# All small parts of the split weights made on VectorE: a one-core layer of attention, RWKV-7 and mixture of experts

## The chip, the cores and the metric

The kernel runs on one core of a Trainium2 chip. TensorE (PE) multiplies, VectorE (DVE), ScalarE (ACT) and GpSimd (POOL) work elementwise, and SyncE (SP) issues most of the transfers from HBM. The metric is the device time of one launch in microseconds (us), lower is better.

## The reference

One layer on 256 tokens of width 1024, in float32:

```python
proj = x @ w_in                                   # 1024 x 5408
y_rwkv = rwkv7_time_mix(token_shift(proj[:, :1824], mu), ...)   # 8 heads of 64, scan over 256 tokens
y_attn = moba_attention(q, k, v)                  # 8 heads of 64, one causal block of 256
mixed = sigmoid(gate_a) * (y_attn @ w_attn_br) + sigmoid(gate_r) * (y_rwkv @ w_rwkv_br)
h = layer_norm(ALPHA * x + mixed @ w_out)
out = layer_norm(ALPHA * h + moe_ffn(h))          # 32 experts, 4 a token, 1024 -> 2048 -> 1024
```

## The kernel before

The kernel has two parts. The **front** (the first 300 us) does everything up to the router. The input projection is cut into twenty chunks of 256 columns, n = 1 to 20 (k, r, v, q and k of the attention, its v, and the two gates), the branch weights into four more, n = 21 to 24. Then the **experts** follow: 32 experts, whose 403 MB of weights are streamed from HBM once, in pieces of 1 MB.

A product of the front is made from three: a weight is split into a large part `hi` (rounded to the type fp32r, line 131, on ScalarE) and a small part `lo`, the rest (line 132, a subtraction of 128x1024). `split(n)` does this in two halves, q = 0 and 1, into one of two pairs of slots in turn, so that chunk n waits until chunk n-2 is multiplied out. `mm3` (lines 140 to 142) multiplies hi by hi, hi by lo and lo by hi: 48 matmuls a chunk. Chunks write two PSUM banks in turn (`b_120` in the rows below is the bank that chunk 8 writes, `b_124` chunk 9, `b_128` chunk 10, `b_132` chunk 11, `b_136` chunk 12, `b_155` chunk 13, `b_159` chunk 14, `b_163` chunk 15, `b_167` chunk 16, `b_188` and `b_192` chunks 19 and 20), and a bank is written again only when its result has been read out: for q and k by lines 562 to 567 on VectorE, for the gates by line 589 on ScalarE. `s_45`, `s_49`, `s_53`, `s_122` and `s_157` are the small parts of chunks 4, 5, 6, 10 and 15; `s_121` and `s_156` are the large parts of chunks 10 and 15.

Beside the chunks run: the inverse of 64 triangular blocks (lines 417 and 419, section `inv`, 31 steps on VectorE, each waiting for the last), its way through HBM and back (lines 423 to 432) to the small products of lines 442 and 449; the recurrence over four pieces of 64 tokens (lines 478 to 508); and the softmax in two halves (lines 600 to 627, the exponentials on line 615).

Which engine makes a small part is read from a table: entry n lists the halves that GpSimd makes, and a chunk without entry has its second half there.

```python
ON_POOL = {6: (0,), 4: (0, 1), 2: (), 21: (0, 1), 14: (0, 1), 8: (0,), 15: (), 1: ()}
```

The order of instructions on each engine is made by a scheduler when the kernel is built, from its own estimate of durations and from the offsets in `PRIORITY`, so that another engine for one instruction changes the order of its neighbours too. On the chip each engine takes its instructions in that order and waits at the first that isn't ready. From the first expert on, TensorE's order is that of the code. `mfill` and `mload` (line 671) ask for expert weights whenever a slot of SBUF is free: the slots of the front become free one after the other, as its last chunks are done, and later each expert's when it has been multiplied.

Of the kernel before, what the change touches and what calls it, by code (L numbers as in the profile page):

```python
# [10 lines left out]
FT = mybir.dt.float32  # L11
# [3 lines left out]
OP = mybir.AluOpType  # L15
# [19 lines left out]

ON_POOL = {6: (0,), 4: (0, 1), 2: (), 21: (0, 1), 14: (0, 1), 8: (0,), 15: (), 1: ()}

# [35 lines left out]
def hybrid_kernel(ctx, tc, xt_d, x_d, win_d, w0_d, ups_d, up2_d, par_d, cA_d, cB_d, wbr_d, wout_d,  # L73
# [7 lines left out]
    V, A, PE, G = nc.vector, nc.scalar, nc.tensor, nc.gpsimd  # L81
    cnt = [0]

    def slot(i, shape, dt=FT):
        cnt[0] += 1
        return slots.tile([128] + shape, dt, name=f"s{i}_{cnt[0]}", tag=f"s{i}")
# [11 lines left out]
    def sec(name):  # L98
        old = cur[0]
        if cur[1] is not None:  # L100
            cur[1].__exit__(None, None, None)
        off = PRIORITY.get(name, 0)
        cur[:] = name, tc.high_priority(offset=off) if off else None
        if off:
            cur[1].__enter__()
        return old
# [5 lines left out]
    RAW, HL = {}, {}  # L112

    def load(n):
        if n >= len(chunks):
            return
        kind, i = chunks[n]
        RAW[n] = slot(raw_of.get(n, raws[n % 2]), [2048])
        src = (win_d if kind == "in" else wbr_d)[i]
        for c in (slice(0, 1024), slice(1024, 2048)) if n == 1 else (slice(0, 2048),):  # L120
            nc.sync.dma_start(RAW[n][:, c], src.rearrange("p a b -> p (a b)")[:, c])

    def split(n):

        if n >= len(chunks):
            return
        hi, lo = slot(hls[2 * n % 4], [2048], FR), slot(hls[2 * n % 4 + 1], [2048], FR)
        old = sec("s%d" % n)
        for q in range(2):
            c = slice(1024 * q, 1024 * q + 1024)  # L130
            A.copy(hi[:, c], RAW[n][:, c])  # L131
            (G if q in ON_POOL.get(n, (1,)) else V).tensor_tensor(lo[:, c], RAW[n][:, c], hi[:, c].bitcast(FT), op=OP.subtract)  # L132
        sec(old)
        a = 8 if chunks[n][0] == "in" else 4
        HL[n] = [t.rearrange("p (a b) -> p a b", a=a) for t in (hi, lo)]
        load(n + 2)
# [50 lines left out]
    for q in range(2):  # L187
        c = slice(4 * q, 4 * q + 4)
# [23 lines left out]


    split(1)
    sec("low")
    pl = [bank(i) for i in range(5)]
# [33 lines left out]
    def proj_chunk(n, b, dst, f0, mc):  # L250
        split(n + 1)
        ps = bank(b, (2, T))
        for h in range(2):
            proj_fm(ps[:, h], n, 128 * h)
            shift(dst[:, f0 + h], ps[:, h], mc + h)
# [4 lines left out]
    for f2 in range(2):  # L260
        pw, pa = bank(2 + 2 * f2, (2, T)), bank(3 + 2 * f2, (2, T))
        for ff in range(2):
            f = 2 * f2 + ff
            c = slice(128 * f, 128 * f + 128)
# [10 lines left out]
    for f in range(4):  # L275
        c = slice(128 * f, 128 * f + 128)
# [161 lines left out]
    for pr in range(2):  # L438
        lo, hi = slice(64 - 64 * pr, 96 - 64 * pr), slice(96 - 64 * pr, 128 - 64 * pr)
# [5 lines left out]
    for pr in range(2):  # L445
        lo, hi = slice(64 - 64 * pr, 96 - 64 * pr), slice(96 - 64 * pr, 128 - 64 * pr)
# [100 lines left out]
    def proj_tok(n, b):  # L547
        split(n + 1)
        ps = bank(b, (2, 256))
        for tt in range(2):  # L550
            tk = slice(128 * tt, 128 * tt + 128)
            for kt in range(8):
                mm3(ps[:, tt], (xh[:, kt, tk], xl[:, kt, tk]), [w[:, kt] for w in HL[n]], kt == 0, kt == 7)
        return ps

    for u in range(4):
# [3 lines left out]
        for tt in range(2):  # L560
            pv = ps[:, tt].rearrange("p (h two d) -> p h two d", two=2, d=32)
            V.tensor_tensor(m1, pv.rearrange("p h two d -> p h (two d)"), cosf[:, tt, None].to_broadcast([128, 4, 64]),
                            op=OP.mult)
            for x in range(2):
                V.tensor_tensor(m2[:, :, x], pv[:, :, 1 - x], sinf[:, tt, None, x].to_broadcast([128, 4, 32]),  # L565
                                op=OP.mult)
# [27 lines left out]
    for h in range(2):  # L594
# [37 lines left out]
        for f2 in range(2):  # L632
            pv = bank(6 + f2, (2, T))
            for ff in range(2):
# [6 lines left out]
                            op=OP.subtract)  # L641
# [59 lines left out]
    for br, (ys_, gt) in enumerate(((yAs, gA), (yRs, gR))):  # L701
        for cc in range(2):
            n = 21 + 2 * br + cc
# [6 lines left out]
            for dd in range(2):  # L710
# [7 lines left out]
                q = slice(2 * d2, 2 * d2 + 2)  # L718
# [407 lines left out]
    for tt in range(2):  # L1126
        zt, st = zs[:, tt], lst[:, tt]
        for n in (1, 0) if tt else (0, 1):
            c = slice(512 * n, 512 * n + 512)
# [63 lines left out]
```

## Time and profile before

| | |
|---|---|
| median of 3 runs | 1225.93 us (1219.89 to 1229.39) |
| profiled execution, its own time | 1228.67 us |
| its span, first to last instruction | 1226.9 us |
| busy: PE, DVE, ACT, POOL | 1144.6, 377.4, 285.9, 66.3 us |
| moved by DMA | 441.08 MB, mean 360 GB/s |

The front and the experts have different limits, so busy shares of the whole span say little; they are read stretch by stretch. Matmuls are pipelined and their ends are modelled, so "busy" for PE means only that something was under way.

### The profile page before, as it was taken

What the parts mean: (1) busy time and instruction counts of PE and PEld (TensorE: products, weight loads), DVE (VectorE), ACT (ScalarE), POOL (GpSimd) and SP (SyncE); (2) the same over time, 40 slices, a digit from 0 to 9 for tenths busy, and PEclk for the clock granted to TensorE, in tenths of its full rate; (3) what the DMA queues carried; (4) which work ended last, traced back from release to release, by engine and by line L of the source; (5) the groups of instructions that cost most, each with busy time, mean ns of one, the idle gap of its engine ahead of it and who ended that gap; (6) DMA issues with size and microseconds to landing.
All of it is one profiled execution on the core that took longest, in us unless ns stands there. A gap on an engine that the chain in (4) does not pass through costs nothing. (4 is left out here: it accounts for less than half of the span.)

```text
span 1226.9 us, 15649 instructions
## 1 busy us (share of the span) xinstructions
PE 1144.6 (93%) x6434; PEld 589.7 (48%) x6434; DVE 377.4 (31%) x786; ACT 285.9 (23%) x566; POOL 66.3 (5%) x40
## 2 busy tenths in 40 slices
PE   8889899999999999999898999999999899999985
PEld 6788888996434344343333343433343333334332
DVE  4787556364222222222212121211212122112114
ACT  5533236644111111111111111111111102111112
POOL 0322221310000000000000000000000000000000
PEclk9997989999999999999999999998999999999998
DMA  7532327886999999999999999999999999999993
GB/s 272 206 87 97 111 69 272 328 330 278 406 422 421 420 420 422 421 421 413 420 421 421 421 421 421 421 421 422 420 421 421 422 422 421 421 421 420 422 418 145
DMA packets 72769, 441.08 MB, mean 360 GB/s; under 512 B 16034, under 2 KB 16562, under 8 KB 20978
## 3 DMA queue, kind: packets, MB, share of 16 engines
q1 hardware_dynamic: 63218, 436.94, 87.3%
q10 hardware_dynamic: 9472, 3.05, 1.0%
q8 instruction: 53, 0.87, 0.3%
q14 instruction: 26, 0.21, 0.0%
HBM read 438.13 MB, written 1.84 MB: 359 GB/s over the span
## 5 line engine op out<-in xcount | busy, mean ns | idle before, releaser
L933 PE MATMUL b<-s,s 128*64 128x512 f32 x2048 | 468.6, 600 | 24.8 <-DMA s<-in_w_dram 24.1
L933 PEld LDWEIGHTS b<-s,s 128*64 128x64 f32 x2048 | 136.4, 137 | 324.6 <-issue 233.8
L916 PE MATMUL b<-s,s 128*64 128x512 f32 x992 | 224.8, 602 | 10.2 <-DMA s<-in_w_dram 5.5
L942 DVE TENSOR_SCALAR s<-b 128x256 f32<-128x256 f32 x64 | 27.2, 424 | 448.5 <-PE b L933 448.5
L916 PEld LDWEIGHTS b<-s,s 128*64 128x64 f32 x992 | 68.6, 138 | 143.1 <-issue 122.9
L140 PE MATMUL b<-s,s 128*128 128x256 f32 (+1 forms) x424 | 127.9, 304 | 7.5 <-DVE s L565 5.5
L142 PE MATMUL b<-s,s 128*128 128x256 f32 (+1 forms) x424 | 128.8, 307 | 3.6 <-DVE s L132 2.5
L141 PE MATMUL b<-s,s 128*128 128x256 f32 (+1 forms) x424 | 127.1, 302 | 0.0
L958 ACT COPY s<-b 128x256 f32<-128x256 f32 x64 | 23.7, 371 | 323.3 <-PE b L953 243.0
L140 PEld LDWEIGHTS b<-s,s 128*128 128x128 f32 x424 | 84.3, 200 | 13.7 <-issue 6.9
L142 PEld LDWEIGHTS b<-s,s 128*128 128x128 f32 x424 | 84.1, 200 | 8.8 <-DVE s L132 3.5
L141 PEld LDWEIGHTS b<-s,s 128*128 128x128 f32 x424 | 84.4, 200 | 3.5 <-issue 2.1
L906 DVE TENSOR_TENSOR s<-b,s 64x512 fp32r<-64x512 f32 (+1 forms) x66 | 44.4, 673 | 125.8 <-ACT s L905 123.4
L905 ACT CAST s<-b 64x512 fp32r<-64x512 f32 (+1 forms) x66 | 37.4, 567 | 194.2 <-PE b L916 181.5
L132 POOL TENSOR_TENSOR s<-s,s 128x1024 fp32r<-128x1024 f32 x24 | 59.9, 2505 | 183.1 <-ACT s L131 147.6
L822 PEld LDWEIGHTS b<-s,s 128*128 128x128 f32 x512 | 58.5, 192 | 13.4 <-issue 12.2
L131 ACT CAST s<-s 128x1024 fp32r<-128x1024 f32 x48 | 49.1, 1045 | 61.6 <-PE b L141 25.6
L822 PE MATMUL b<-s,s 128*128 128x128 f32 x512 | 61.9, 278 | 0.9 <-DVE s L816 0.9
L943 ACT ACTIVATE s<-s 128x256 f32<-128x256 f32 x64 | 26.9, 421 | 146.4 <-DVE s L942 146.3
L1133 POOL TENSOR_TENSOR s<-s,s 128x512 f32<-128x512 f32 x2 | 2.9, 1426 | 965.1 <-ACT s L1131 965.1
L929 PE MATMUL b<-b1r,pick 128*128 128x512 f32 x128 | 45.9, 440 | 0.0
L816 DVE TENSOR_TENSOR s<-cA,rt 128x128 f32<-128x128 f32 x32 | 9.0, 287 | 104.6 <-PE b L857 104.6
(266 smaller groups left out, 864.6 us busy)
## 6 DMA issues: line engine op xcount, KB each, us to landing
s<-in_w_dram SPq DMA_DIRECT2D x380, 1024.0 KB, 19.8
s<-in_win_dram SPq DMA_DIRECT2D x19, 1024.0 KB, 5.1
s<-in_wbr_dram SPq DMA_DIRECT2D x4, 1024.0 KB, 6.5
s<-in_wout_dram SPq DMA_DIRECT2D x4, 1024.0 KB, 4.8
s<-in_w2l_dram SPq DMA_DIRECT2D x7, 512.0 KB, 16.6
s<-in_xt_dram SPq DMA_DIRECT2D x4, 256.0 KB, 4.7
s<-in_win_dram SPq DMA_DIRECT2D x2, 512.0 KB, 7.1
s<-in_x_dram ACTq DMA_DIRECT2D x1, 1024.0 KB, 9.8
```

The source lines that it names most:

```text
L131: A.copy(hi[:, c], RAW[n][:, c])
L132: (G if q in ON_POOL.get(n, (1,)) else V).tensor_tensor(lo[:, c], RAW[n][:, c], hi[:, c].bitcast(FT), op=OP.subtract)
L140: PE.matmul(ps, lhs[0], rhs[0], start=first, stop=False)
L141: PE.matmul(ps, lhs[0], rhs[1], start=False, stop=False)
L142: PE.matmul(ps, lhs[1], rhs[0], start=False, stop=last)
L822: PE.matmul(pg[h][:, d % 4], xtok[:, tt, 128 * d:128 * d + 128], oh[:, tt], start=tt == 0 and d % 4 == 0, stop=tt == 1 and d % 4 == 3)
L905: A.copy(hi, ps)
L906: V.tensor_tensor(lo, ps, hi.bitcast(FT), op=OP.subtract)
L916: PE.matmul(ps[64 * n:64 * n + 64], aTs[e % 2][:, b, hf, 64 * g_:64 * g_ + 64], w[:, hf, 512 * n:512 * n + 512], start=ft == 0, stop=ft == 7)
L929: PE.matmul(ps, pick, b1r[:, x], start=x == 0, stop=False)
L933: PE.matmul(ps[64 * g_:64 * g_ + 64], XG[:, kt, 64 * j:64 * j + 64], w[:, kt % 2, 512 * g_:512 * g_ + 512], start=False, stop=kt == 7)
L942: V.tensor_scalar(gl, pv[:, :, 0], 7.0, None, op0=OP.min)
```

## The change

The table is deleted, and every small part of the 24 chunks is made on VectorE; the large parts stay on ScalarE. Of the 48 subtractions 24 were on VectorE, and 24 move there from GpSimd. What is computed stays the same.

```diff
-ON_POOL = {6: (0,), 4: (0, 1), 2: (), 21: (0, 1), 14: (0, 1), 8: (0,), 15: (), 1: ()}
...
             A.copy(hi[:, c], RAW[n][:, c])
-            (G if q in ON_POOL.get(n, (1,)) else V).tensor_tensor(lo[:, c], RAW[n][:, c], hi[:, c].bitcast(FT), op=OP.subtract)
+            V.tensor_tensor(lo[:, c], RAW[n][:, c], hi[:, c].bitcast(FT), op=OP.subtract)
```

Two lines fewer stand ahead of the rest, so line 132 of before is line 130 of the changed kernel, and so on. The order changes on all engines in the front; three places follow.

**Chunks 4 and 5, VectorE.** Between the shifts of k (line 210, now 208), before:

```order
L305 TENSOR_SCALAR s_24_175<-s_20_171,par 128x256
L210 SCALAR_TENSOR_TENSOR s_19_170<-b_36_269,par,s_19_170 128x255
L289 TENSOR_SCALAR s_22_173<-s_19_170,par 128x256
L210 SCALAR_TENSOR_TENSOR s_19_170<-b_47_409,par,s_19_170 128x255
L305 TENSOR_SCALAR s_24_175<-s_20_171,par 128x256
L306 TENSOR_TENSOR s_19_170<-s_19_170,s_24_175 128x1024
L132 TENSOR_TENSOR s_49_463<-s_35_267,s_48_462 128x1024
L294 TENSOR_SCALAR s_2_70<-s_2_70 8x256
```

and now:

```order
L303 TENSOR_SCALAR s_24_175<-s_20_171,par 128x256
L130 TENSOR_TENSOR s_45_402<-s_27_182,s_44_401 128x1024
L208 SCALAR_TENSOR_TENSOR s_19_170<-b_36_269,par,s_19_170 128x255
L130 TENSOR_TENSOR s_45_402<-s_27_182,s_44_401 128x1024
L287 TENSOR_SCALAR s_22_173<-s_19_170,par 128x256
L208 SCALAR_TENSOR_TENSOR s_19_170<-b_47_409,par,s_19_170 128x255
L130 TENSOR_TENSOR s_49_463<-s_35_267,s_48_462 128x1024 x2
L292 TENSOR_SCALAR s_2_70<-s_2_70 8x256
```

Three subtractions that stood on GpSimd now stand on VectorE, ahead of lines 303 to 306.

**Chunks 8 and 10, VectorE, within the inverse.** The bank of chunk 8, `b_120`, is read out (lines 562 to 567); before:

```order
L562 TENSOR_TENSOR s_112_1140<-b_120_1214,s_7_100 128x256
L419 TENSOR_TENSOR s_70_710<-s_70_710,s_84_798 64x12x20
L132 TENSOR_TENSOR s_122_1272<-s_115_1147,s_121_1271 128x1024
L417 TENSOR_TENSOR s_84_798<-s_70_710 64x231
L565 TENSOR_TENSOR s_112_1140<-b_120_1214,s_7_100 128x4x32
L419 TENSOR_TENSOR s_70_710<-s_70_710,s_84_798 64x11x21
L565 TENSOR_TENSOR s_112_1140<-b_120_1214,s_7_100 128x4x32
```

and now:

```order
L560 TENSOR_TENSOR s_112_1140<-b_120_1214,s_7_100 128x256
L415 TENSOR_TENSOR s_84_798<-s_70_710 64x192
L130 TENSOR_TENSOR s_122_1272<-s_115_1147,s_121_1271 128x1024
L417 TENSOR_TENSOR s_70_710<-s_70_710,s_84_798 64x8x24
L130 TENSOR_TENSOR s_122_1272<-s_115_1147,s_121_1271 128x1024
L415 TENSOR_TENSOR s_84_798<-s_70_710 64x175
L563 TENSOR_TENSOR s_112_1140<-b_120_1214,s_7_100 128x4x32
L417 TENSOR_TENSOR s_70_710<-s_70_710,s_84_798 64x7x25
L563 TENSOR_TENSOR s_112_1140<-b_120_1214,s_7_100 128x4x32
```

Both halves of chunk 10's small part now stand ahead of the two reads that empty the bank, four steps of the inverse later. On TensorE the first matmul of chunk 10 (`b_128`) stood behind chunk 9, before:

```order
L140 MATMUL b_124_1279<-s_117_1206,s_8_109 128x256
L141 MATMUL b_124_1279<-s_118_1207,s_8_109 128x256
L142 MATMUL b_124_1279<-s_117_1206,s_9_110 128x256
L140 MATMUL b_128_1344<-s_121_1271,s_8_109 128x256
L141 MATMUL b_128_1344<-s_122_1272,s_8_109 128x256
```

and stands straight behind chunk 8 now, which uses the same bank:

```order
L138 MATMUL b_120_1214<-s_113_1141,s_8_109 128x256
L139 MATMUL b_120_1214<-s_114_1142,s_8_109 128x256
L140 MATMUL b_120_1214<-s_113_1141,s_9_110 128x256
L138 MATMUL b_128_1344<-s_121_1271,s_8_109 128x256
L139 MATMUL b_128_1344<-s_122_1272,s_8_109 128x256
```

**The first softmax, ScalarE and VectorE.** On ScalarE the large part of chunk 15 stood behind all eight exponentials, before:

```order
L615 ACTIVATE s_145_1546,smst<-s_145_1546,smst 128x256
L615 ACTIVATE s_145_1546,smst<-s_145_1546,smst 128x128
L615 ACTIVATE s_145_1546,smst<-s_145_1546,smst 128x256
L131 CAST s_156_1651<-s_135_1465 128x1024
L480 COPY s_91_950<-b_107_1092 64x512
L131 CAST s_156_1651<-s_135_1465 128x1024
L627 COPY s_112_1140<-b_149_1575 128x4x128
```

and now in their middle (line 613 is the exponential, 129 the large part):

```order
L613 ACTIVATE s_145_1546,smst<-s_145_1546,smst 128x128
L613 ACTIVATE s_145_1546,smst<-s_145_1546,smst 128x256
L129 CAST s_156_1651<-s_135_1465 128x1024 x2
L613 ACTIVATE s_145_1546,smst<-s_145_1546,smst 128x128
L613 ACTIVATE s_145_1546,smst<-s_145_1546,smst 128x256
L613 ACTIVATE s_145_1546,smst<-s_145_1546,smst 128x128
L613 ACTIVATE s_145_1546,smst<-s_145_1546,smst 128x256
L587 ACT_TABLE_LOAD
L587 ACTIVATE s_142_1542<-b_159_1659 128x512
```

On VectorE both halves of chunk 15's small part now stand right ahead of the softmax's division (lines 615 to 617, before 617 to 619), and TensorE's transposes of the result (line 621, before 623) stand straight behind the last matmul of chunk 13 (`b_155`):

```order
L140 MATMUL b_155_1601<-s_8_109,s_134_1460 128x256
L621 MATMUL b_149_1575<-cA,s_145_1546 128x128 x4
L138 MATMUL b_167_1775<-s_8_109,s_160_1709 128x256
L621 MATMUL b_150_1581<-cA,s_145_1546 128x128 x4
L139 MATMUL b_167_1775<-s_9_110,s_160_1709 128x256
```

Chunk 15 uses the slots of chunk 13, so its cast waits for that chunk's last matmul.

## Rows read from the trace of the kernel before

**Rows 1.** The page, part 2: 40 slices of 30.7 us of the span.

```profile
DMA  7532327886999999999999999999999999999993
GB/s 272 206 87 97 111 69 272 328 330 278 406 422 421 420 420 422 421 421 413 420 421 421 421 421 421 421 421 422 420 421 421 422 422 421 421 421 420 422 418 145
```

**Rows 2.** Windows: us; busy PE, PEld, DVE, ACT, POOL; PE clock, DMA share, GB/s.

```profile
70.00:143.00 73.00, 63.40 (x507) 59.27 (x504) 56.47 (x121) 21.59 (x29) 16.34 (x7) 0.91 0.35 108
...
195.00:290.00 95.00, 94.77 (x683) 86.16 (x681) 52.14 (x86) 48.68 (x72) 22.88 (x9) 1.00 0.80 312
...
310.00:1195.00 885.00, 836.55 (x4170) 331.04 (x4168) 182.19 (x423) 141.88 (x338) 0.00 (x0) 0.99 1.01 421
```

**Rows 3.** SP's own waits from 230 to 310 us: total, times, longest, in us.

```profile
SPq L671 <- PE b L142: 16.2, 2, 11.9
```

**Rows 4.** Line 132: count, min/median/max in ns, first and last start.

```profile
L132 DVE TENSOR_TENSOR s<-s,s x24: 1195/1222/3370, 14.5 to 250.9; 128x1024 fp32r<-128x1024 f32 x24
L132 POOL TENSOR_TENSOR s<-s,s x24: 2350/2436/3275, 30.0 to 251.9; 128x1024 fp32r<-128x1024 f32 x24
```

**Rows 5.** Timeline, VectorE: start and duration in us, line, operation, idle time before.

```profile
30.12 2.48 DVE L305 TENSOR_SCALAR s<-s,par 128x256 f32<-128x256 f32 x1
...
37.84 0.41 DVE L305 TENSOR_SCALAR s<-s,par 128x256 f32<-128x256 f32 x1 [1.41 <-PE b L291]
...
88.77 2.43 DVE L419 TENSOR_TENSOR s<-s,s 64x207 f32<-64x207 f32 x1
```

**Rows 6.** Timeline, GpSimd, 0 to 310 us.

```profile
29.96 2.48 POOL L132 TENSOR_TENSOR s<-s,s 128x1024 fp32r<-128x1024 f32 x1 [27.80 <-ACT s L131]
...
88.47 2.50 POOL L132 TENSOR_TENSOR s<-s,s 128x1024 fp32r<-128x1024 f32 x1 [5.49 <-ACT s L131]
```

**Rows 7.** Waits of TensorE, 28 to 70 us: total, times, longest.

```profile
PE b L142 <- DVE s L132: 2.5, 3, 1.9
PE b L142 <- POOL s L132: 1.2, 2, 0.6
```

**Rows 8.** Waits of TensorE, 70 to 146 us.

```profile
PE b L140 <- DVE s L565: 5.5, 4, 1.6
PE b L392 <- DVE s L210: 2.1, 1, 2.1
PE b L442 <- DMA s<-tblk: 0.9, 1, 0.9
PE b L140 <- DVE s L210: 0.9, 1, 0.9
```

**Rows 9.** Windows cut at changes of the PE clock, and chunk 15 alone (last).

```profile
58.90:62.30 3.40, 3.40 (x18) 3.40 (x17) 3.40 (x7) 0.14 (x1) 0.00 (x0) 0.50 0.00 0
93.00:106.60 13.60, 13.60 (x91) 12.24 (x90) 5.35 (x14) 4.89 (x10) 0.95 (x1) 0.50 0.23 78
...
151.10:157.90 6.80, 6.80 (x55) 6.34 (x54) 1.54 (x3) 4.48 (x8) 6.02 (x3) 0.50 0.44 154
171.70:178.50 6.80, 6.80 (x27) 5.38 (x26) 3.91 (x8) 1.57 (x2) 0.00 (x0) 0.51 0.00 0
195.00:200.76 5.76, 5.76 (x50) 5.71 (x48) 3.77 (x8) 2.22 (x3) 0.00 (x0) 1.00 0.83 303
```

**Rows 10.** Timeline, VectorE, inside the inverse: first and last of 14 instructions.

```profile
125.06 0.27 DVE L565 TENSOR_TENSOR s<-b,s 128x128 f32<-128x128 f32 x1
...
128.17 0.26 DVE L419 TENSOR_TENSOR s<-s,s 64x112 f32<-64x112 f32 x1
```

**Rows 11.** Timeline, ScalarE: table load, first and last of eight exponentials, a cast.

```profile
180.83 1.28 ACT L615 ACT_TABLE_LOAD   x1
182.12 0.40 ACT L615 ACTIVATE s<-s,smst 128x128 f32<-128x128 f32 x1
...
185.55 0.19 ACT L615 ACTIVATION_READ_ACCUMULATOR s<-s,smst 128x1 f32 x1
189.00 1.05 ACT L131 CAST s<-s 128x1024 fp32r<-128x1024 f32 x1 [3.26 <-PE b L141]
```

## The prediction

> **What bounds the kernel now.** I read the slices of the page first: the transfers run at 420 GB/s in nearly every slice from the twelfth on, and far below that before [rows 1]. The windows say the same: from 310 to 1195 us the DMA share is 1.01, so the experts are bound by the stream of weights and nothing on VectorE or GpSimd matters there [rows 2]. The question is what fixes the moment from which the stream is full. In the last 95 us of the front the DMA share is only 0.80 [rows 2], and SP's own waits say why: its loads of expert weights (line 671) wait 16.2 us for the front's matmuls to give up slots [rows 3]. So I take it that a front that ends x us later or earlier moves the end of the kernel by x us, and that nothing is won back later.
>
> The front itself is bound by TensorE, with gaps. A chunk of 48 matmuls takes 5.76 us at full clock [rows 9], the 24 chunks are therefore some 138 us, and the rest is small products. From 195 to 290 us TensorE is busy 94.77 of 95 us, from 70 to 143 us 63.4 of 73 us [rows 2]. Gaps and half clock are what a change of the elementwise engines can touch. The reader should see in the rows that the gaps are few and known by name: 3.7 us for small parts before 70 us [rows 7], 9.4 us after it, of which 5.5 us because VectorE had not emptied a bank [rows 8]; and that the clock stands at 0.50, so at 1.2 instead of 2.4 GHz, in four stretches of 3.4, 13.6, 6.8 and 6.8 us [rows 9], each of which costs half its length where TensorE has no slack. The first two come behind TensorE's longest waits, of 1.9 us and 2.1 us [rows 7, 8]; the last comes behind no wait, only behind many small products.
>
> **The change, part by part.** *The work itself.* 24 subtractions of 2.4 us leave GpSimd, and 24 of 1.2 us come to VectorE [rows 4]. That is not 29 us more for VectorE. While GpSimd subtracts, VectorE stands: line 305, which takes 0.41 us alone, took 2.48 us exactly while GpSimd's subtraction ran, and a step of the inverse took 2.43 us [rows 5, 6]. There are eleven such stretched instructions between 30 and 135 us, beside eleven subtractions on GpSimd; they last 20 us longer than their like, and the same subtractions on VectorE cost 11 x 1.2 = 13 us. VectorE wins 7 us there. The Trainium skill says the same of the mechanism (SBUF — State Buffer, Who interferes with whom: GpSimd and a VectorE instruction with two SBUF inputs exclude each other for a whole instruction). It does not say who waits for VectorE, and the trace alone decides that.
>
> *Chunks 2 to 6 (28 to 70 us).* The small parts of chunks 4 and 5 come one after the other on VectorE, 1.2 us each, instead of 2.4 us on GpSimd with VectorE's own half stuck behind. I let all 3.7 us of waits go [rows 7], and with the longest of them the half-clock stretch from 58.9 us, 3.4 / 2 = 1.7 us [rows 9]. What is late next is VectorE's chain to the score matmuls, in which chunk 6 now has two subtractions instead of one held up: I put a new wait of 2 us there (bounds 0 and 2.4, two subtractions). Together -3.4 us, bounds -5.4 and 0.
>
> *Chunks 7 to 12 and the inverse (70 to 143 us).* The 9.4 us of waits [rows 8] belong to the old order; I take them all out and put those of the new order in. There, TensorE goes from chunk 8 straight to chunk 10, which uses the same bank. VectorE empties that bank only behind both subtractions of chunk 10, and these wait for ScalarE's cast into the slots of chunk 8. From chunk 8's last matmul that is: two casts, 2 x 1.05 [rows 11], the last subtraction, 1.2 [rows 4], and the twelve instructions down to the last read, at 3.1 us for 13 steps or 0.24 us each [rows 10], 2.9 us. Sum 6.2 us with TensorE idle, where before 48 matmuls of chunk 9 stood between. Chunk 11 then waits in the same way for the bank of chunk 9, whose reads stand ten instructions on: 12 x 0.24 less 17 matmuls of 0.12 us, about 1.0 us; and the small products behind the trip of the inverse through HBM come to be asked for some 1.5 us early. New waits: 8.7 us, bounds 3 (if VectorE has slack in front of chunk 10) and 12. The half-clock stretch of 13.6 us from 93 us costs 6.8 us. The wait of 2.1 us ahead of it goes, but the transposes and 64-row products that fill it stay; between all and nothing I take half, -3.4 us. Behind the wait of 6.2 us I expect a new stretch, the shortest seen, 3.4 us, so +1.7. Together -9.4 + 8.7 - 3.4 + 1.7 = -2.4 us.
>
> *The recurrence and the first softmax (143 to 195 us).* A subtraction of chunk 13 now stands ahead of the first copy of the recurrence (line 485): +1.2 us, one subtraction, bounds 0 and 2.4. The dear place is the softmax. Half of its exponentials stand on ScalarE behind the casts of chunk 15, which wait for the last matmul of chunk 13, and TensorE's next instruction is a transpose of the softmax's result. After that last matmul: two casts, 2.1; four exponentials, half of the 3.6 us that eight took, 1.8; then a table load, 1.3 [rows 11], a read-out of a bank, 0.6 (512 columns, about half a cast), another cast, 1.05, a copy and a second read-out, 1.2, until the bank of chunk 15 is free. Laid end to end on ScalarE, with the division beside it on VectorE, that is 8.0 us, in which TensorE has about 1.3 us of matmuls. I take +6.7 us, bounds 3 and 8. Where the exponentials stand before the casts, as now, this costs nothing. Half clock behind it: one stretch of 6.8 us, +3.4. Together +11.3 us.
>
> *Gates, branches and output (195 to 290 us).* TensorE is full here. Where GpSimd's half came after 2.4 us, both halves come after 2 x 1.2, so the hand-over takes as long, and a chunk's 5.76 us cover it. One place is worse: chunk 20 now begins after 12 matmuls of chunk 19 instead of 46, and its bank waits on ScalarE for three casts (line 535 is the third) and the read-out, 3 x 1.05 + 0.6 = 3.7 us, of which 12 x 0.12 are covered: +2.3 us.
>
> *GpSimd and the transfers.* GpSimd keeps some fills and two products at the very end, which don't change: nothing there. Loads of gate and branch weights change places on SP; a chunk's load is asked for one chunk ahead, so I cost that at nothing, and at one load of 1 MB, 2.5 us at 420 GB/s [rows 1], if it fails.
>
> Sum: -3.4 - 2.4 + 11.3 + 2.3 = **+7.8 us**, on 1228.67 us of the profiled execution. That execution is 2.7 us above the median of the three runs; on the median it is 1225.9 + 7.8, so **1233 us**, 0.6% slower. A measurement of this kernel can tell about 1% from no change, so this counts as none.
>
> **The rivals.** *All relief, no new wait.* VectorE's 7 us are won and the new waits are covered, because the casts and reads come before TensorE needs them: -3.7 - 1.7 - 9.4 - 6.8 = -21.6 us, 1204 us. For it speaks the stretched steps of the inverse [rows 5]; against it the new order on TensorE, which has no other work at the two places. The Trainium skill (GPSIMD Engine Reference, Engine selection) would have this: elementwise work with two inputs belongs on VectorE, GpSimd being about twice as slow. The rows agree on the ratio, 2436 to 1222 ns [rows 4], and not on the result, since the waits are those of banks and slots. Chance 0.10.
>
> *Cold.* The two long waits put TensorE to half clock for as long as the stretch from 93 us, 13.6 us each, so 6.8 us instead of 1.7 and 3.4, and that stretch itself stays (+3.4): 7.8 + 5.1 + 3.4 + 3.4 = +19.7 us, 1246 us, slower. It decides from the moment that small products follow the wait, as they do at 93 us; for it speaks that the recurrence and the transposes come right after both waits. Against it: the stretch from 58.9 us, behind a wait of 1.9 us, ended after 3.4 us because full chunks followed [rows 9]. Chance 0.25.
>
> *Nothing.* The front's end is hidden by the stream, or gains and waits cancel: 1226 us. For it speaks that the stream is full for 885 us; against it that its start waits for the front's slots [rows 3]. Chance 0.12.
>
> **How the numbers follow.** My forecast has the remaining 0.53. Faster by over 1% (under 1213.7) needs most of the first rival: 0.08. Slower by over 1% (above 1238.2) comes from the cold rival, 0.22 of its 0.25, and from the upper bounds of the waits, 0.05: 0.27. The rest, 0.65, is within 1%. For the range I leave out the first rival and the end of the cold one: from 1218 (forecast with the long waits at their lower bounds and the stretch at 93 us gone: 1233 - 5.7 - 3.7 - 3.4, about 1220, and 2 for the spread of the runs) to 1248 (the cold rival and the same spread).
>
> **What would show it.** In the profile of the changed kernel: no subtraction on GpSimd, and no VectorE instruction in the inverse above 1.3 us; TensorE waiting some 6 us for line 563 (565 of before) once, instead of 1.3 us four times, and some 5 us or more around line 621 for ScalarE and VectorE; the full stream beginning about 8 us later. Wrong I would be if the transposes' wait is short, because chunk 13 ends earlier against the exponentials than I laid it out, or if the clock stays up: then the result falls below 1226. If the start of the full stream and the end of the kernel move by different amounts, the first step is wrong.

## The result and the profile after

The changed kernel takes 1232.87 us (median of 20 runs, 1228.43 to 1240.64), the kernel before 1226.3 us (20 runs, 1216.33 to 1231.7). The ratio is 1.0061, interval 1.0042 to 1.0079: slower by some 0.6%. A ratio of 1 lies outside the interval, but the difference is less than the 1% that the prediction counts as a change. The forecast was 1233 us.

The two profiled executions differ by far less, 1229.62 to 1228.67 us: that of after lies 3.2 us under its median, that of before 2.4 us over. So this pair of traces shows what moved, and the size of the loss rests on the medians. First the slices of the page of after (as [rows 1]):

```profile
PEclk8998899999999999999999999998999999999998
DMA  7535254876999999999999999999999999999993
GB/s 272 206 86 159 83 205 171 308 312 252 412 421 420 420 421 422 421 420 414 421 420 421 422 421 421 421 420 421 421 422 421 422 420 421 420 421 421 421 417 124
```

The stream is as full as before, from the same slice on. The prediction had it begin about 8 us later, and in this pair it doesn't: the first gate product behind the router begins at 304.4 us, in before at 304.5. The windows of after (columns as in [rows 2]), and below them the two of before that [rows 2] leaves out:

```profile
28.00:70.00 42.00, 39.95 (x293) 32.76 (x292) 32.63 (x51) 22.62 (x37) 0.98 (x2) 1.00 0.49 177
70.00:143.00 73.00, 65.17 (x634) 61.61 (x631) 53.20 (x130) 26.43 (x38) 0.96 (x1) 0.88 0.39 111
143.00:195.00 52.00, 47.10 (x397) 41.75 (x395) 31.70 (x51) 24.17 (x43) 0.00 (x0) 0.93 0.42 159
195.00:290.00 95.00, 92.13 (x645) 83.38 (x644) 58.02 (x95) 43.76 (x66) 0.00 (x0) 0.98 0.74 286
310.00:1195.00 885.00, 837.65 (x4168) 332.03 (x4164) 182.04 (x423) 141.99 (x338) 0.00 (x0) 0.99 1.01 421
```

```profile
28.00:70.00 42.00, 38.27 (x253) 31.25 (x253) 32.24 (x42) 22.05 (x36) 13.22 (x7) 0.96 0.47 166
143.00:195.00 52.00, 51.31 (x506) 45.39 (x506) 24.72 (x43) 24.80 (x45) 9.38 (x4) 0.84 0.34 110
```

From them a ledger of the front between 28 and 290 us can be made. TensorE's idle time is length less busy time; what the clock takes is (1 - clock) x length. Before: idle 3.7 + 9.6 + 0.7 + 0.2 = 14.2 us, clock 1.7 + 6.6 + 8.3 + 0 = 16.6 us, sum 30.8. After: idle 2.0 + 7.8 + 4.9 + 2.9 = 17.6 us, clock 0 + 8.8 + 3.6 + 1.9 = 14.3 us, sum 31.9. (Where TensorE stands still at half clock, the second term counts too much.) By stretch, after less before is -3.4, +0.4, -0.5 and +4.5 us, together 1.1. The windows are cut by time, not by work. Gains and losses nearly cancel: waits moved from many small ones to a few long ones, and half clock moved with them.

VectorE did win what was promised, and more. Lines 417 and 419 of before are 415 and 417 now (minimum, median and maximum in ns, first and last start):

```profile
L130 DVE TENSOR_TENSOR s<-s,s x48: 1204/1220/1227, 15.3 to 250.2; 128x1024 fp32r<-128x1024 f32 x48
L415 DVE TENSOR_TENSOR s<-s x31: 168/352/411, 80.1 to 117.3; 64x31 f32<-64x31 f32 x2, 64x60 f32<-64x60 f32 x2, 64x87 f32<-64x87 f32 x2, 64x112 f32<-64x112 f32 x2
L417 DVE TENSOR_TENSOR s<-s,s x31: 170/349/418, 80.5 to 117.6; 64x31 f32<-64x31 f32 x2, 64x60 f32<-64x60 f32 x2, 64x87 f32<-64x87 f32 x2, 64x112 f32<-64x112 f32 x2
```

No step of the inverse is above 418 ns now, where one took 2.43 us beside GpSimd [rows 5, 6]. The last step begins at 117.6 us; in before it began at 134.8:

```profile
L419 DVE TENSOR_TENSOR s<-s,s x31: 176/353/2428, 83.2 to 134.8; 64x31 f32<-64x31 f32 x2, 64x60 f32<-64x60 f32 x2, 64x87 f32<-64x87 f32 x2, 64x112 f32<-64x112 f32 x2
```

So the inverse ends 17 us earlier, and yet the kernel isn't faster. TensorE's waits of after, from 28, 70 and 146 us on (as [rows 7, 8]), show where TensorE stands still now:

```profile
PE b L331 <- ACT s L280: 1.1, 1, 1.1
...
PE b L138 <- DVE s L563: 6.8, 1, 6.8
PE b L489 <- ACT s L129: 0.9, 1, 0.9
...
PE b L621 <- DVE s L616: 4.8, 1, 4.8
PE b L138 <- ACT s L587: 2.3, 1, 2.3
```

These are the bank of chunk 10, the softmax and the bank of chunk 20. The windows cut at changes of the clock (as [rows 9]):

```profile
110.20:120.30 10.10, 5.50 (x26) 5.53 (x27) 9.06 (x33) 0.00 (x0) 0.00 (x0) 0.50 0.65 225
134.00:140.90 6.90, 6.01 (x56) 5.47 (x53) 6.21 (x8) 5.27 (x8) 0.00 (x0) 0.51 0.45 154
178.40:185.20 6.80, 3.91 (x17) 3.49 (x18) 5.60 (x8) 6.75 (x16) 0.00 (x0) 0.50 0.66 242
226.00:229.60 3.60, 3.60 (x20) 3.60 (x20) 1.10 (x1) 0.00 (x0) 0.00 (x0) 0.53 0.67 225
```

The first, the third and the fourth belong to the three waits. The stretch from 93 us is gone altogether.

### The profile page after: what moved, and what is told of

The parts are those of the page before. It is cut to its first block, busy times and chain, and to the rows that moved or that the text cites. A ratio compares the mean times of both kernels' runs of the same rounds, so it can differ in the third digit from the quotient of the medians.

```text
span 1227.9 us, 15590 instructions
## 1 busy us (share of the span) xinstructions
PE 1141.8 (93%) x6434; PEld 588.0 (48%) x6434; DVE 385.1 (31%) x810; ACT 284.0 (23%) x565; POOL 6.4 (1%) x16
## 5 line engine op out<-in xcount | busy, mean ns | idle before, releaser
L138 PEld LDWEIGHTS b<-s,s 128*128 128x128 f32 x424 | 84.5, 199 | 17.3 <-issue 10.1
L130 DVE TENSOR_TENSOR s<-s,s 128x1024 fp32r<-128x1024 f32 x48 | 58.0, 1219 | 22.3 <-ACT s L129 21.9
L825 ACT ACTIVATE s<-b,par 128x128 f32<-128x128 f32 x64 | 29.3, 457 | 45.7 <-DVE s L827 45.6
```

The source lines that it names most:

```text
L130: V.tensor_tensor(lo[:, c], RAW[n][:, c], hi[:, c].bitcast(FT), op=OP.subtract)
L138: PE.matmul(ps, lhs[0], rhs[0], start=first, stop=False)
L825: A.activation(dst, src, AF.Identity, scale=pc(P_G1 + d), bias=pc(P_B1 + d))
```

## The experiments

Every ratio is to runs of the kernel before on the same chip, whose medians were 1227.88 us (early, middle, late, longer front), 1227.21 (early and late, softmax, own bank, three remedies) and 1225.8 us (the last four: gate bank, wait filled, three on before, chunk 8 first); "front" is the start of line 857 (855 of after), the first gate product behind the router, in the profiled execution.

| run | median us | ratio to before (95%) | front, span of its profile |
|---|---|---|---|
| before | 1226.3 | | 304.5, 1226.9 |
| after | 1232.87 | 1.0061 (1.0042 to 1.0079) | 304.4, 1227.9 |
| early alone | 1225.54 | 1.0008 (0.9974 to 1.0042) | 299.1, 1224.3 |
| middle alone | 1233.24 | 1.0050 (1.0027 to 1.0073) | 308.0, 1231.5 |
| late alone | 1232.34 | 1.0054 (1.0031 to 1.0078) | 302.6, 1228.5 |
| early and late | 1230.19 | 1.0021 (1.0003 to 1.0039) | 306.0, 1229.4 |
| longer front | 1240.53 | 1.0128 (1.0088 to 1.0168) | 312.0, 1235.3 |
| softmax first | 1222.02 | 0.9960 (0.9942 to 0.9979) | 290.5, 1214.9 |
| own bank | 1217.08 | 0.9911 (0.9884 to 0.9939) | 292.3, 1218.0 |
| gate bank | 1228.35 | 1.0031 (1.0008 to 1.0054) | 301.4, 1226.7 |
| three remedies | 1215.34 | 0.9896 (0.9869 to 0.9923) | 290.2, 1215.3 |
| wait filled | 1232.55 | 1.0066 (1.0042 to 1.0089) | 302.0, 1229.9 |
| three on before | 1235.56 | 1.0082 (1.0051 to 1.0113) | 302.8, 1228.4 |
| chunk 8 first | 1216.01 | 0.9931 (0.9908 to 0.9954) | 295.6, 1221.1 |

My theory: the order of instructions sets the time, through TensorE's waits at three places and the clock behind them. The rivals: only VectorE's work counts, or nothing of the front reaches the end.

**Is the front's end the kernel's end?** Before, with more to multiply:

```diff
+                    if n >= 23:
+                        for kt in range(4):
+                            c0 = 256 * dd + 128 * d
+                            mm3(ps[:, d], ...)
```

> Before, with the products of the branch chunks 23 and 24 made twice (the second time over the first, so the output stays): 96 matmuls of 0.12 us more, 11.5 us of TensorE, with no other order. By my first step (the front's end moves the kernel's end one to one): +11.5 us. By the rival that the stream hides the front's end: 0 to +3 us.

Measured: 12.7 us more on the medians of that chip (1227.88 before), by the ratio 15.7 (10.8 to 20.6); 11.5 were expected. Over the 14 profiles of the table a line through span against front rises by 0.91 us per us, and the spans lie 1.3 us from it (standard deviation; the largest distance is 3.2 us, in wait filled). So the first step holds within some 3 us: little of the front is hidden. Part of the distance arises at the very end. In before and after the fronts end together, but the second product of the last expert (line 916, 914 of after) begins at 1194.25 us in before and at 1196.23 us in after, and TensorE stands still ahead of it for 4.6 and 7.3 us.

**The change in parts.** One condition each:

```diff
-(G if q in ON_POOL.get(n, (1,)) else V)
+(G if q in ON_POOL.get(n, (1,)) and not 1 <= n <= 6 else V)     # early
+(G if q in ON_POOL.get(n, (1,)) and not 7 <= n <= 12 else V)    # middle
+(G if q in ON_POOL.get(n, (1,)) and not 13 <= n <= 24 else V)   # late
+(G if q in ON_POOL.get(n, (1,)) and 7 <= n <= 12 else V)        # early and late
```

> Of before, only the small parts of chunks 1 to 6 go to VectorE; from chunk 7 on TensorE has before's order. By my terms (the order decides through waits and clock): the 3.7 us of waits and the half-clock stretch of 3.4 us before 70 us go, a wait of about 2 us comes, so -3.4 us against before (0 to -5.4). By the rival that only VectorE's freed time counts: -5 us or more, since GpSimd's blocking in the first 70 us is gone. By the rival that nothing of the front reaches the end: 0.

The waits for small parts go, from 3.7 [rows 7] to 0.3 us, by the waits of this run from 28 to 70 us:

```profile
PE b L333 <- ACT s L282: 1.1, 1, 1.1
PE b L142 <- DVE s L132: 0.3, 1, 0.3
```

The time doesn't follow: the ratio, 1.0008 (0.9974 to 1.0042), shows no change, and the -3.4 us lie just outside its interval, while the medians differ by 2.3 us in favour of this run. Its profile has two stretches at half clock between 28 and 70 us, 6.8 us together, where before has one of 3.4. The first score product (line 392) begins at 78.1 us here and at 81.0 in before, but with other executions counted the orders don't differ: 78.1 to 82.0 us in five with before's order of the first 70 us, 78.1 to 82.0 in nine with that of after.

> Of before, only the small parts of chunks 7 to 12 go to VectorE. The scheduler then puts chunk 10 straight behind chunk 8 on TensorE and two of eight exponentials ahead of the casts of chunk 15, as in the changed kernel. By my terms: -2.4 us for the middle, +10.1 us for the softmax and the clock behind it, together about +8 us, with one wait of TensorE of 6 to 7 us for line 565 and one of about 5 us at line 623. By the rival of VectorE's freed time: the inverse ends some 15 us earlier and the time falls by 7 to 16 us.

Measured +0.50% (1.0027 to 1.0073), some 6 us, close to my terms (+8). Its waits are those of after, from 70 and from 146 us on:

```profile
PE b L140 <- DVE s L565: 6.8, 1, 6.8
...
PE b L623 <- DVE s L618: 5.8, 1, 5.8
```

The inverse ended nearly as early as in after (the last step, line 419 here, begins at 119.9 us; in after, line 417, at 117.6), so VectorE's work gained what the rival said, and the kernel lost.

> Of before, only the small parts of chunks 13 to 24 go to VectorE; up to chunk 12 and for the exponentials the order is before's. By my terms: +1.2 us for line 485 behind a subtraction and +2.3 us at the bank of chunk 20, so +3.5 us, and no long wait at line 623. By the rival of VectorE's freed time: 0, since TensorE is full from 195 us on.

Measured +0.54%, 6.6 us (3.8 to 9.6), above my 3.5, which lies just under the interval. Another wait than mine is there: chunk 20's bank costs nothing in this order, but the transposes of the second softmax wait (from 195 us on):

```profile
PE b L623 <- DVE s L618: 1.2, 1, 1.2
PE b L623 <- ACT s L627: 1.2, 1, 1.2
```

The rest of the loss isn't explained. In its profile the front ended 2 us before that of before, so what is lost there is lost behind the front: the second product of the last expert (line 916) begins at 1196.25 us, 2 us later than in before, TensorE having stood still for 7.4 us until a transfer of weights had landed. Why that transfer came late stays open.

> Of before, the small parts of chunks 1 to 6 and 13 to 24 go to VectorE, those of 7 to 12 stay as before. If effects add up (early alone came out near -1, late alone near +5): +4 us against before. If the loss of the late part was one of clock in those executions, and not of its order: -1 us.

Measured +0.21%, 2.6 us (0.4 to 4.8): the +4 of the expectation lies inside, the -1 outside. By their ratios the two parts alone would make 7.6 us, so part of what late alone lost isn't found here. The same two waits of 1.2 us stand at line 623.

**The three waits undone.** Each of these edits changes the order of other instructions too. Gains against after are differences of medians; after was set against other runs of before than these were, and by the ratios the gains of the softmax, the own bank, the gate bank and all three are 12.4, 18.4, 3.7 and 20.2 us. First the softmax, in after:

```diff
-'sm0': -27,
+'sm0': 60,
```

> The changed kernel with another priority of the first softmax (sm0 60 for -27): all eight exponentials stand ahead of the casts of chunk 15, nothing else moves before that place or in the late part. If the casts among the exponentials are what TensorE waits for at the transposes (4.8 us in the changed kernel), that wait falls under 2 us, chunk 15 waits some 2 us for its own split, and the time falls by 3 to 8 us against the changed kernel (8 with the half-clock stretch behind the wait). If the wait only goes on to chunk 15: 0.

The time falls by 10.9 us against after, above the 3 to 8 expected, to 0.4% below before. The wait at the transposes falls to 0.7 us, and from 143 to 195 us the clock is at full:

```profile
PE b L621 <- DVE s L616: 0.7, 1, 0.7
...
143.00:195.00 52.00, 50.11 (x431) 45.03 (x431) 36.03 (x57) 28.38 (x48) 0.00 (x0) 1.00 0.47 169
```

One thing I had expected wrongly: the priority moves the score products too. The scores' first read (line 599) begins at 154.6 us instead of 162.1, and the first exponential at 164.45 instead of 173.97. So this run doesn't price the casts between the exponentials, but the whole late softmax. That the casts stood in the way in after is seen in ScalarE's timeline of after:

```profile
175.26 0.49 ACT L613 ACTIVATE s<-s,smst 128x256 f32<-128x256 f32 x1
175.66 0.19 ACT L613 ACTIVATION_READ_ACCUMULATOR s<-s,smst 128x1 f32 x1
176.43 1.99 ACT L129 CAST s<-s 128x1024 fp32r<-128x1024 f32 x2 [0.59 <-PE b L139]
178.33 0.40 ACT L613 ACTIVATE s<-s,smst 128x128 f32<-128x128 f32 x1
...
180.00 0.18 ACT L613 ACTIVATION_READ_ACCUMULATOR s<-s,smst 128x1 f32 x1
```

TensorE's idle time begins at 176.5 us, with the casts, and ends at 181.3, behind the division.

Then the bank of chunk 10, in after:

```diff
-        ps = proj_tok(7 + u, u % 2)
+        ps = proj_tok(7 + u, 6 if u == 3 else u % 2)
```

> The changed kernel with chunk 10 in a bank of its own (6 for 1). If the bank behind VectorE's reads is what costs at chunk 10, the wait of 6.8 us there becomes one of about 2.3 us, for half a split (a cast of 1.05 and a subtraction of 1.2), and with the half clock behind it 4.5 to 9 us are won against the changed kernel; the scheduler also puts seven of eight exponentials ahead of chunk 15's casts, worth some 5 us more by the same theory. If only VectorE's amount of work counts: 0, since that stays.

The time falls by 15.8 us against after, above the 9.5 to 14 that the two parts of the expectation make. The wait for VectorE's reads is gone; what is late next is chunk 10's split:

```profile
PE b L138 <- ACT s L129: 2.5, 2, 1.7
PE b L139 <- DVE s L130: 0.9, 1, 0.9
```

Though only chunk 10's bank was edited, the waits of 4.8 us at the first transposes and of 2.3 us at chunk 20's bank are gone too: from 70 to 290 us no wait of TensorE is longer than 1.7 us. So this run prices the three waits together and not the bank alone. VectorE still makes all 48 subtractions, so the rival that only its amount of work counts (0) is wrong.

The bank of chunk 20, in after:

```diff
-        ps = bank(j % 2, (2, T))
+        ps = bank(2 if j == 7 else j % 2, (2, T))
```

> The changed kernel with only chunk 20 in another bank (2 for 1). If the wait of 2.3 us for ScalarE's read-out is that of the bank, it goes and 2 us are won, at most 4 with the half clock behind it. If chunk 20's own split comes no earlier: 0.

The wait of 2.3 us is gone, and with it the half clock behind it: 4.5 us on the medians (1232.87 to 1228.35), where the wait and half of the stretch of 3.6 us come to 4.1. The intervals of the two ratios overlap (1.0008 to 1.0054, and 1.0042 to 1.0079), so the size is uncertain.

All three together:

> The changed kernel with all three waits attacked: chunk 10 in bank 6, chunk 20 in bank 2 and the softmax's priority at 60. If the three waits (6.8, 4.8 and 2.3 us) and the clock behind them are the loss, 10 to 17 us are won against the changed kernel, so 1216 to 1223 us, faster than before by 3 to 10 us. If the clock falls anyway, or the waits only move: within 4 us of the changed kernel.

1215.34 us, just under the range expected, 17.5 us below after and 1.0% below before: the lowest median of this study. Its windows from 28 to 290 us:

```profile
28.00:70.00 42.00, 40.43 (x287) 33.47 (x287) 32.49 (x50) 22.63 (x37) 0.98 (x2) 0.96 0.49 176
70.00:143.00 73.00, 66.45 (x643) 62.48 (x639) 51.93 (x128) 26.07 (x36) 0.95 (x1) 0.95 0.38 109
143.00:195.00 52.00, 50.53 (x448) 43.90 (x447) 38.04 (x61) 28.82 (x51) 0.00 (x0) 1.00 0.49 183
195.00:290.00 95.00, 92.01 (x654) 80.56 (x653) 56.23 (x106) 44.47 (x70) 0.00 (x0) 1.00 0.79 302
```

The ledger: idle 12.6, clock 5.3, sum 17.9 us, against 30.8 of before. The difference of 12.9 us is close to what the medians show (12 us on this chip, 1227.21 to 1215.34). The gains of the three edits alone, 10.9, 15.8 and 4.5 us, add up to 31 and not to 17.5, since each edit alone moves other waits as well. The own bank alone (0.9884 to 0.9939) can't be told apart from all three (0.9869 to 0.9923).

**Do the remedies need the change?** The same three edits on before, GpSimd kept:

> The three remedies of the run with three on the kernel before, GpSimd's subtractions kept (chunk 10 in bank 6, chunk 20 in bank 2, sm0 60). If moving the subtractions is worth something once its waits are gone, this stays above 1222 us, since chunk 10 waits little for its bank here and the inverse stays long; if the remedies alone make the gain, it comes to 1215 to 1219 us.

Slower than before. The reads of line 565 still hold TensorE for 4.5 us, and with the softmax moved ahead, the small products have few chunk matmuls among them. The wait, and one stretch of this run:

```profile
PE b L140 <- DVE s L565: 4.5, 2, 3.1
...
136.00:153.00 17.00, 17.00 (x199) 16.08 (x198) 1.54 (x3) 7.52 (x12) 7.01 (x3) 0.50 0.37 92
```

So the edits are no gain by themselves. No run keeps before's order while the subtractions move, so what the moved work alone is worth stays open: that VectorE's freed time is worth the whole 20 us between the two runs with three remedies isn't shown, since their orders and clocks differ.

**Is it the standing still that costs clock, and does the clock cost time?** In after, ahead of chunk 10's products:

```diff
+        if n == 10:
+            fl_ = bank(7, (2, 256))
+            for i in range(40):
+                PE.matmul(fl_[:, 0], HL[n][0][:, 0, 0:128], xh[:, 0], start=True, stop=True)
```

> The changed kernel with 40 needless matmuls (4.8 us at full clock, into a bank that nobody uses then) behind the first cast of chunk 10, inside TensorE's wait of 6.8 us; chunk 10's bank and all of VectorE's order stay. If the clock falls because TensorE stands still there, the half-clock stretch of some 10 us behind the wait goes and about 5 us are won against the changed kernel, though no work is saved. If the clock falls for another reason: 0, or up to 2 us lost where the matmuls reach past the wait.

The trace says yes to the first question, for this stretch. The needless matmuls (line 551) stand in the wait, and the stretch that ran at half clock in after is at full clock:

```profile
109.53 5.05 PE L551 MATMUL b<-s,s 128*128 128x256 f32 x40 [1.45 <-ACT s L129]
```

The windows of this run:

```profile
110.20:120.30 10.10, 10.04 (x83) 9.65 (x82) 9.41 (x33) 0.23 (x1) 0.00 (x0) 1.00 0.64 220
132.80:139.50 6.70, 5.57 (x47) 5.00 (x46) 5.22 (x6) 4.70 (x8) 0.00 (x0) 0.50 0.44 157
159.80:163.40 3.60, 3.60 (x34) 3.15 (x34) 2.07 (x4) 0.00 (x0) 0.00 (x0) 0.53 0.00 0
```

In all four profiles with this wait left empty (after, middle, softmax and gate bank), half clock begins inside it and lasts 6.8 to 10.1 us. The time shows no gain: 1232.55 us, where 5 were expected. Of the 10.1 us at half clock in after, 4.6 lay in the wait; the rest cost 2.75 us, and a gain of that size is too small for these runs (their intervals reach 2.3 and 2.9 us to either side). So the second question stays open. Of the 2.75 us, little reaches the softmax: its transposes begin at 180.9 us instead of 181.3, behind the same wait of 4.8 us and one new stretch at half clock.

**Another order instead of another bank.** In after, chunk 8 ahead of chunk 9:

```diff
-PRIORITY = {..., 'sm0': -27, ...}
+PRIORITY = {'qk1': 300, ..., 'sm0': 60, ...}
-        ps = bank(j % 2, (2, T))
+        ps = bank(2 if j == 7 else j % 2, (2, T))
```

> The changed kernel with chunk 8 ahead of chunk 9 on TensorE (priority qk1 300), the exponentials ahead of chunk 15 (sm0 60) and chunk 20 in bank 2; banks of chunks 8 and 10 as in the changed kernel. With 32 other instructions between chunk 8 and chunk 10, the bank and the split of chunk 10 are covered: the wait of 6.8 us goes without a new bank, and the time falls to that of the run with three remedies or some 3 us below it, 1212 to 1217 us. If the small products of the recurrence, now bare of chunk matmuls in places, bring the clock down: 1218 to 1226 us.

1216.01 us, about as fast as with the banks (the ratio, 0.9931, puts it a little behind): the wait for line 563 is 0.2 us here. In its place TensorE waits for small parts (line 130) twice, 3.9 us together, and the clock is at 0.50 in two stretches of 6.8 us from 122 and 142 us. Its profile is of the slowest of its six runs, 1222.87 us.

## Why the prediction was right, point by point

*The bound* (the front's end moves the kernel's end): right within some 3 us, by the run with the longer front and by the line through 14 profiles. The sign named for it, a stream that begins about 8 us later, isn't in the pair of profiles, which differ by 1.0 us in all.

*The work.* GpSimd's blocking is real: the 62 steps of the inverse take 20.3 us of VectorE instead of 32.6, and it ends 17 us earlier. (The 7 us of the prediction were VectorE's net gain, so the two don't compare.) In after and in middle alone this made the kernel no faster: the small products behind the inverse come earlier, but TensorE's sum of work stays.

*Chunks 2 to 6.* Predicted -3.4, measured nothing (ratio 1.0008). The failed step is the credit for the half clock: "with the longest of them the half-clock stretch" was to go, but that wait had ended at 53.2 us, 5.7 us ahead of the stretch, and such stretches come in the first 70 us under either order. From 0 to 70 us the mean clock is 0.93 to 1.00 in five profiles with before's order there, and 0.88 to 0.95 in nine with that of after. From 28 to 70 us it is 1.00 in the profile of after, but 0.88 to 0.96 in the eight others with its order: that profile was a lucky one.

*Chunks 7 to 12.* The wait of 6.2 us was measured as 6.8, from the chain as laid out. The other new waits were put at 2.5 (the 1.0 in it is 0.8 by its own terms) and came to 0.9. Half of the stretch from 93 us was to stay; all of it went. That isn't the order's doing alone: late alone and three on before have the same wait of 2.1 us and behind it before's order on TensorE, and from 93.0 to 106.6 us their clock is at 1.00 (125 and 115 matmuls begin there, where before has 91 at 0.50). Behind the wait came a stretch of 10.1 us, of which 5.5 cost clock (2.75 us; predicted 1.7), and one of 6.9 us that I had not listed. With the softmax, the middle alone was put at about +8 and measured at about +6.

*The softmax.* Predicted a wait of 6.7 and half clock worth 3.4, measured 4.8 and 2.0: the stretch has the 6.8 us as put, but TensorE was busy for 3.9 of them only. The last part of my chain, the read-out and copy up to chunk 15's bank, didn't hold TensorE up, and the 1.2 us for line 485 are in no wait of after. What the sum left out is larger. Before has three stretches at half clock from 143 to 195 us, the two of 6.8 us and one of 3.4 us from 144 us, which the prediction's list of four lacks; after has one, and none was counted as going. So by the ledger this part cost -0.5 us, where +11.3 was put. Undoing the late softmax won 10.9 us, since that brings the scores forward too.

*Late.* The 2.3 us at chunk 20's bank are there to the tenth. Undoing them won 4.5 us, since half clock behind them had not been counted; late alone, with another wait in its place, cost more than its term too. The loads of gate and branch weights, put at nothing, are in no wait of TensorE in the front of after.

*The rivals.* "All relief" at 1204 us was wrong for this change: the new waits weren't covered. With the three waits gone the same moved work gives 1215 us, so part of its relief is there to be had. Of "cold", the clock did fall behind both long waits, for 10.1 and 6.8 us instead of 13.6, and what had been there before went. "Nothing", by cancelling, is near the ledger of the two profiles (+1.1 us); over all runs a ratio of 1 lies outside the interval.

The waits were laid out rightly, two of the three to within 0.6 us, but the right total has much luck in it. The terms -3.4, -2.4, +11.3 and +2.3 stand against -3.4, +0.4, -0.5 and +4.5 in the ledger of the two profiles, +1.1 in all, and against +6.6 us on the medians. The mean granted clock of after's 20 runs is 0.969, that of 73 runs of before 0.973; by the line of the last section, some 3 us of the 6.6 go with that. Which stretches these are, and where the rest arises, one profile a side doesn't show.

## What to carry to other kernels

Where a scheduler makes the order, moving work to the faster engine is two changes, less work and another order. Read from the new order where a bank or slot is taken again with nothing in between, and price that chain instruction by instruction: this gave 6.2 for 6.8 us and 2.3 for 2.3, and 6.7 for 4.8 where the chain was taken too far. The clock behind such waits wasn't to be had that way. If such a wait eats the gain, give the place its own bank or another priority before giving up the move; three such edits turned +0.6% into -1.0%, and one of them alone, the bank of chunk 10, into -0.9%. Edits that change the order don't add up, so they are measured together.

## What the runs showed of the hardware that was not expected

*The same program's time goes with its clock.* Over 73 runs of before, the mean granted clock goes from 0.967 to 0.982 and the time from 1232 to 1217 us: a line of -836 us per unit, correlation -0.87, rest 1.8 us. A hundredth of mean clock is 8.4 us here, more than the effect of this change, so that one profile a side says little about half a per cent. The Trainium skill (TensorE: Matmul & The Clock Gate, What's actually happening) says of a kernel's start that the same kernel shows different numbers of slow matmuls from run to run, and advises against fitting to a count. These runs agree in kind, with mean clocks of 0.967 to 0.982, and the differences aren't at the start alone: from 93 us on, profiles with the same wait of 2.1 us ahead have 13.6 us at 0.50 or none, as told above.

*Half clock also comes with a busy TensorE.* In the run with three remedies on before it fell behind a wait of 2.6 us (line 442, for a transfer) and then stood at 0.50 for 17 us, with TensorE busy for all of them (199 matmuls, small products among them): work alone didn't bring it back there.
